# PEER layer on one core: the experts of the first 128 tokens gathered row by row, the dense products run for the other 384

## Chip, cores, metric

One core of one Trainium2 chip. The time is the device time of one execution in microseconds. The kernel before took a median of 5038.12 us over three runs (5035.39 to 5038.38).

## What is computed

Two macaron transformer layers, a mixer of gated delta rule and mLSTM, and then a PEER layer, on 512 tokens of width 1024. The change touches only the PEER layer, which scores product keys, picks 16 experts for each of 8 heads and each token (128 of 16384 experts for a token), and sums their outputs:

```python
def _peer(h, w_q, sub_keys, u_tab, v_tab):          # h: [1, 512, 1024]; u_tab, v_tab: [16384, 1024]
    qry = (t @ w_q).reshape(n_tok, 8, 2, 128)
    scores = jnp.einsum("thpd,hpkd->thpk", qry, sub_keys)              # 128 keys in each half
    s_top, i_top = lax.top_k(scores, 16)
    cand = (s_top[:, :, 0, :, None] + s_top[:, :, 1, None, :]).reshape(n_tok, 8, -1)
    cand_idx = (i_top[:, :, 0, :, None] * 128 + i_top[:, :, 1, None, :]).reshape(n_tok, 8, -1)
    best, pos = lax.top_k(cand, 16)
    idx, gate = jnp.take_along_axis(cand_idx, pos, axis=-1), jax.nn.softmax(best, axis=-1)
    # per block of 128 tokens (tb, ib, gb):
    act = jax.nn.gelu(jnp.einsum("td,thkd->thk", tb, u_tab[ib]), approximate=False)
    out = jnp.einsum("thk,thkd->td", gb * act, v_tab[ib])
```

## The kernel before

Activations lie transposed: eight tiles `x[m]` of 128 features by 512 tokens. Every product with weights goes through `lin` (line 93): one 512 KB load of weights on SyncE's queue (`raw`, 3 buffers), a split into a high and a low float32r part (`wh` by ScalarE at line 82, `wl` by VectorE at line 83, 3 buffers each), and 24 matmuls of 128x128 weights against 512 columns (8 slices of the depth, and for each high by high, high by low, low by high), collected in one PSUM bank. Below, a **lin** is one such set of 24 matmuls.

The PEER layer runs in three stretches.

- **Keys** (`topk`, lines 1481 to 1493): 16 lins for the queries, the key scores, and VectorE's search for the top 16.
- **Pairs** (lines 1497 to 1553): for each of four tiles of 128 tokens, the top 16 of 256 sums for each head, the two key numbers and the gate of each pair (`res`), and then the gate matrix: for each token a 128x128 product of two one-hot tiles (`lt` by VectorE, `rt` by ScalarE and GpSimd), copied by ScalarE into `stage` and stored to DRAM as `gate_d`, so that a token's 16384 gates are zero except at its experts. While this goes on, the first 32 of the 128 blocks of 128 experts have their activations computed ahead (`ahead`, one lin each) and left in DRAM.
- **Dense** (lines 1442 to 1469): 16 groups of 8 expert blocks, 4 to 15 first and then 0 to 3. For each block one lin against `pu`, then VectorE multiplies by 1/rms (`t`, line 1428), ScalarE applies gelu (line 1430), GpSimd multiplies by the gates (`act`, line 1456), ScalarE and VectorE split the product (`eh`, `el`, 11 buffers). For each of 8 output tiles one lin against `pv` with these as moving operand, and VectorE adds the result to `x` (line 1464). The last four groups load their activations and need only the 8 `pv` lins.

In all 128 `pu` and 128 `pv` lins. Each engine runs its instructions in the order of one list; a scheduler draws up that list from program order, so the lists, not the source, tell what stands behind what.

## Time and profile before

| | us |
|---|---|
| median of 3 runs | 5038.12 |
| span of the profiled execution, first to last instruction | 5030.3 |
| around the span (the median less the span; the profiled execution has no time of its own beside the span) | 7.8 |
| TensorE busy in the span | 4827.2 |
| PEER, keys (3300 to 3415) | 115 |
| PEER, pairs (3415 to 3800) | 385 |
| PEER, dense (3800 to 5014) | 1214 |
| final norm and store (5014 to 5030) | 16 |

The stages are cut by hand where the lines of the chain that ended last change from one part of the code to the next. Busy time of TensorE counts matmuls that overlap, each with a modelled end, so a high share says that it is never without work, and the distance between starts says how fast it goes.

### The profile page before, as it was taken

To read this page: it belongs to the slowest core of one execution; us is meant where nothing else is said; L and a number is where in the kernel's file an instruction comes from. 1 tells how busy PE (TensorE), PEld (TensorE's weight loads), DVE (VectorE), ACT (ScalarE), POOL (GpSimd) and SP (SyncE) were. 2 spreads that over 40 slices of the span, in tenths; PEclk is the share of its full clock that TensorE was granted. 3 is DMA by queue.
4 is the path that set the end of the run, shared out by engine and by line. 5 is a ranking of instruction groups with operands and counts; after the bars stand their busy time and mean duration, and the time that the engine had idled before them with its cause. 6 is when DMAs were issued, how large, how long until landed. Compare 5 with 4: busy or idle time off the path is not lost. (4 is left out here: it accounts for less than half of the span.)

```text
span 5030.3 us, 63501 instructions
## 1 busy us (share of the span) xinstructions
PE 4827.2 (96%) x23313; PEld 3957.2 (79%) x23313; DVE 3015.1 (60%) x5922; ACT 2024.4 (40%) x3525; POOL 917.8 (18%) x868
## 2 busy tenths in 40 slices
PE   9999989999999999899999989888899999999998
PEld 7888777788888887777887878767677888888887
DVE  4457877644544587876444678679884444344454
ACT  3235556522322365564223323226784323232332
POOL 0001022200000010223001012234662112121132
PEclk9999999999999999999999999999999999999999
DMA  3334233533323342325233331333445433334353
GB/s 126 96 112 132 78 96 85 174 93 95 100 93 96 113 128 75 106 86 168 94 96 114 115 120 35 99 98 132 149 169 164 130 113 117 126 113 130 113 194 99
DMA packets 256981, 575.05 MB, mean 114 GB/s; under 512 B 28224, under 2 KB 96480, under 8 KB 252576
## 3 DMA queue, kind: packets, MB, share of 16 engines
q1 hardware_dynamic: 256672, 570.99, 35.9%
q8 instruction: 186, 3.05, 0.2%
q14 instruction: 123, 1.01, 0.1%
HBM read 469.31 MB, written 78.53 MB: 109 GB/s over the span
## 5 line engine op out<-in xcount | busy, mean ns | idle before, releaser
L82 ACT CAST wh<-raw 128x1024 fp32r<-128x1024 f32 (+3 forms) x773 | 766.9, 993 | 1964.9 <-PE bk L101 1450.8
L101 PE MATMUL bk<-hh,wh 128*128 128x512 f32 x3016 | 1191.6, 395 | 12.8 <-ACT hh L225 9.2
L101 PE MATMUL bk<-hh,wl 128*128 128x512 f32 x3016 | 1189.6, 394 | 1.7 <-POOL wl L83 1.5
L101 PE MATMUL bk<-hl,wh 128*128 128x512 f32 x3016 | 1188.4, 394 | 0.3 <-DVE hl L226 0.3
L83 DVE TENSOR_TENSOR wl<-raw,wh 128x1024 fp32r<-128x1024 f32 (+3 forms) x693 | 822.3, 1188 | 140.1 <-ACT wh L82 133.2
L101 PEld LDWEIGHTS bk<-hh,wh 128*128 128x128 f32 x3016 | 571.5, 189 | 130.4 <-ACT hh L225 9.6
L101 PEld LDWEIGHTS bk<-hh,wl 128*128 128x128 f32 x3016 | 570.5, 189 | 118.1 <-POOL wl L83 1.9
L101 PEld LDWEIGHTS bk<-hl,wh 128*128 128x128 f32 x3016 | 571.1, 189 | 116.4 <-issue 2.4
L101 PE MATMUL bk<-eh,wh 128*128 128x512 f32 x1024 | 403.0, 394 | 2.8 <-ACT eh L90 2.8
L101 PE MATMUL bk<-el,wh 128*128 128x512 f32 x1024 | 403.5, 394 | 0.8 <-DVE el L91 0.5
L101 PE MATMUL bk<-eh,wl 128*128 128x512 f32 x1024 | 400.1, 391 | 0.0
L1456 POOL TENSOR_TENSOR act<-act,gt 128x512 f32<-128x512 f32 x128 | 224.2, 1759 | 955.1 <-ACT act L1430 813.6
L191 POOL TENSOR_TENSOR sq<-sq,sqt 128x512 f32<-128x512 f32 x62 | 103.7, 1673 | 1212.2 <-ACT sqt L187 1192.0
L1464 DVE TENSOR_TENSOR x<-bk,x 128x512 f32<-128x512 f32 x128 | 88.4, 691 | 371.1 <-PE bk L101 371.1
L83 POOL TENSOR_TENSOR wl<-raw,wh 128x1024 fp32r<-128x1024 f32 (+2 forms) x80 | 185.7, 2322 | 575.4 <-ACT wh L82 455.8
L101 PE MATMUL bk<-gh,wh 128*128 128x512 f32 x704 | 274.4, 390 | 0.0
L101 PE MATMUL bk<-gl,wh 128*128 128x512 f32 x704 | 274.3, 390 | 0.0
L101 PE MATMUL bk<-gh,wl 128*128 128x512 f32 x704 | 274.3, 390 | 0.0
L101 PEld LDWEIGHTS bk<-eh,wh 128*128 128x128 f32 x1024 | 193.0, 188 | 46.3 <-ACT eh L90 3.6
L101 PEld LDWEIGHTS bk<-el,wh 128*128 128x128 f32 x1024 | 193.2, 189 | 43.4 <-DVE el L91 3.2
L101 PEld LDWEIGHTS bk<-eh,wl 128*128 128x128 f32 x1024 | 192.8, 188 | 42.4
L250 DVE TENSOR_TENSOR t<-bk,rr 128x512 f32<-128x512 f32 x88 | 60.8, 691 | 269.1 <-PE bk L101 269.1
(681 smaller groups left out, 8339.5 us busy)
## 6 DMA issues: line engine op xcount, KB each, us to landing
raw<-in_wi SPq DMA_DIRECT2D x176, 512.0 KB, 3.7
raw<-in_pu SPq DMA_DIRECT2D x128, 512.0 KB, 3.5
raw<-in_pv SPq DMA_DIRECT2D x128, 512.0 KB, 3.6
gate_d<-stage SPq DMA_DIRECT2D x32, 1024.0 KB, 3.9
gt<-gate_d SPq DMA_DIRECT2D x16, 2048.0 KB, 9.7
raw<-in_wo SPq DMA_DIRECT2D x64, 448.0 KB, 3.3
raw<-in_mg SPq DMA_DIRECT2D x48, 512.0 KB, 3.7
raw<-in_wo SPq DMA_DIRECT2D x32, 512.0 KB, 3.5
```

The source lines that it names most:

```text
L82: self.nc.scalar.copy(wh[:, :n], raw[:, :n])
L83: (eng or self.nc.vector).tensor_sub(wl[:, :n], raw[:, :n], wh[:, :n].bitcast(F))
L101: self.nc.tensor.matmul(ps, x[:, c], y[k], start=(n == 0), stop=(n == 3 * kk - 1))
L191: nc.gpsimd.tensor_add(self.sq, self.sq, t)
L250: nc.vector.tensor_mul(t2, pb, rr)
L1456: nc.gpsimd.tensor_mul(av, av, gt[:, :, e, :])
L1464: nc.vector.tensor_add(self.x[m], ps, self.x[m])
```

## The change

The first tile of 128 tokens leaves the dense path. `SPT` is 128 and `DW` is 384, the columns that stay.

- Every `pu` and `pv` lin has 384 moving columns in place of 512, and so have `t`, `act`, `eh`, `el`, the gate tile `gt`, the stored activations and the addition to `x`. The weights, their loads and their splits stay as they are: 256 lins, 512 KB each.
- No gate matrix is built for the first tile: its 32 steps of `rt`, `lt`, four matmuls and a copy to `stage`, and its stores, are gone. In their place its expert numbers are written as integers (`eidx`) beside the gates (`egate`). The `ahead` calls that hung on that tile's blocks go with them, so that 26 lins are asked for during the pairs and 6 after them, where it was 30 and 2.
- `by_token` writes the normed activations of those tokens with a token on each partition (`ht`, 128x1024): ScalarE copies, eight transposes.
- `gathered` runs through the 128 experts of each token in steps of four: four indirect DMAs on GpSimd's queue fetch for each token its row of `pur` (128 rows of 4 KB, 512 KB in all), VectorE multiplies each with `ht` and sums (`dot`), ScalarE applies gelu to the four, VectorE multiplies by the gates, then four more indirect DMAs fetch the rows of `pvr` and VectorE adds each, scaled, to `acc`. All 256 fetched tiles `er` share 4 buffers. The tables `pur` and `pvr` are new inputs in the reference's own layout.
- In the last group `acc` is transposed and added to the first 128 columns of `x`.

```diff
-                ps = self.lin(a["pu"][j], 8, hh, hl, eng)
-                t1 = mp.tile([128, 512], F, name="t1", bufs=2)
-                nc.vector.tensor_mul(t1, ps, rr)
-                act = mp.tile([128, 512], F, name="act", bufs=4)
+                ps = self.lin(a["pu"][j], 8, hh, hl, eng, cols=dn)
+                t1 = mp.tile([128, DW], F, name="t1", bufs=2)
+                nc.vector.tensor_mul(t1, ps, rr[:, dn])
+                act = mp.tile([128, DW], F, name="act", bufs=4)
...
+    def gathered(self, ht):
+        nc, mp, a = self.nc, self.mp, self.a
+        NB = 4
+        acc = mp.tile([128, D], F, name="acc")
...
+        def fetch(table, s):
+            r = mp.tile([128, D], F, name="er", tag="er", bufs=4)
+            nc.gpsimd.indirect_dma_start(r, None, a[table], bass.IndirectOffsetOnAxis(ap=self.eidx[:, s:s + 1], axis=0))
+            return r
+        for b in range(0, 128, NB):
+            dot = mp.tile([128, NB], F, name="dot", bufs=2)
+            for i in range(NB):
+                r = fetch("pur", b + i)
+                nc.vector.tensor_tensor_reduce(out=r, in0=r, in1=ht, scale=1.0, scalar=0.0, op0=OP.mult, op1=OP.add,
+                                               accum_out=dot[:, i:i + 1])
+                if i == NB - 1:
+                    w = mp.tile([128, NB], F, name="ew", bufs=2)
+                    nc.scalar.activation(w, dot, AF.Gelu)
+                    nc.vector.tensor_mul(w, w, self.egate[:, b:b + NB])
+                yield
+            for i in range(NB):
+                r = fetch("pvr", b + i)
+                nc.vector.scalar_tensor_tensor(acc, r, w[:, i:i + 1], acc, op0=OP.mult, op1=OP.add)
+                yield
...
                         wh.append(h)
                         wl.append(q)
+                        more(0 if last else 2 if e % 4 == 0 else 1)
+                    if g == groups[-2]:
+                        more(256)
                     for m in range(8):
...
-                        ps = self.lin(a["pv"][g, m], 8, wh, wl)
-                        nc.vector.tensor_add(self.x[m], ps, self.x[m])
-                        if g == groups[-1]:
+                        ps = self.lin(a["pv"][g, m], 8, wh, wl, cols=slice(0, DW))
+                        x = self.x[m][:, dn]
+                        nc.vector.tensor_add(x, ps[:, 0:DW], x)
+                        more(0 if g >= groups[-2] else 1)
...
+            if s0 < 0:
+                nc.vector.scalar_tensor_tensor(res[0], res[0], 128.0, res[1], op0=OP.mult, op1=OP.add)
+                nc.vector.tensor_copy(self.eidx, res[0].rearrange("p h k -> p (h k)"))
+                nc.vector.tensor_copy(self.egate, g.rearrange("p h k -> p (h k)"))
+                continue
```

`more(n)` takes n steps of `gathered`. In program order that is 18 fetches for each group of 8 blocks. The engines' lists are denser: by VectorE's list 12 of the 256 fetched tiles are used before the last `lt` of the pairs, and then 30 for each group of 8 `pu` and 8 `pv` lins, so that all are used up a little past the eighth group and the rest of the dense stretch has none.

VectorE's list in the pairs of the first tile, from the gates of its pairs on, before (line 1525 writes the normed gates, line 1530 copies the transposed lists, line 1549 makes `lt`):

```order
L1525 TENSOR_TENSOR res_30291<-res_30291,gz 128x128 [waits DVE_49]
L83 TENSOR_TENSOR wl<-raw,wh 128x1024 [waits DMAHW5_49]
L1530 COPY sel_28978<-pt 128x128 [waits PE_49]
L1530 COPY sel_28979<-pt 128x128
L1530 COPY sel_28980<-pt 128x128
L1532 TENSOR_SCALAR sel_28981<-pt 128x128
L1549 TENSOR_SCALAR lt<-io,sel_28978,sel_28980 128x128 [waits DVE_49]
L1549 TENSOR_SCALAR lt<-io,sel_28978,sel_28980 128x128 x3
L1428 TENSOR_TENSOR t_30433<-bk,rr 128x512 [waits Activation_49]
L83 TENSOR_TENSOR wl<-raw,wh 128x1024 [waits DMAHW7_49,Activation_49]
```

The same place in the changed kernel (lines 1606 to 1608 write the expert numbers and the gates; line 1486 is `t` of a lin ahead, line 1414 the search of the next tile):

```order
L1608 COPY egate<-res_30329 128x128 [waits DVE_49]
L1607 CAST eidx<-res_30327 128x128 [waits DVE_49]
L1486 TENSOR_TENSOR t_30384<-bk,rr 128x384 [waits PE_49]
L1486 TENSOR_TENSOR t_30420<-bk,rr 128x384 [waits PE_49]
L85 TENSOR_TENSOR wl<-raw,wh 128x1024 [waits DMAHW3_49,Activation_49]
L1414 MAX best<-cand 128x8 [waits Pool_49]
L1414 MAX best<-cand 128x8
```

The copies and the 128 `lt` of the first tile are gone, and the search for the next tile follows at once.

VectorE's list in the middle of the dense stretch, before, at a run of `pv` lins (line 1464 adds a finished lin to `x`, line 83 splits the weights of a later one; the brackets name the semaphores waited for):

```order
L1464 TENSOR_TENSOR x<-bk,x 128x512 [waits PE_49]
L83 TENSOR_TENSOR wl<-raw,wh 128x1024 [waits DMAHW5_49,DVE_49,Activation_49]
L1464 TENSOR_TENSOR x<-bk,x 128x512 [waits PE_49]
L83 TENSOR_TENSOR wl<-raw,wh 128x1024 [waits DMAHW6_49,DVE_49,Activation_49]
L1464 TENSOR_TENSOR x<-bk,x 128x512 [waits PE_49]
L83 TENSOR_TENSOR wl<-raw,wh 128x1024 [waits DMAHW0_49,Activation_49]
L1464 TENSOR_TENSOR x<-bk,x 128x512 [waits PE_49]
```

The same kind of place in the changed kernel (line 1535 is the addition, line 85 the split, lines 1450 and 1459 use a fetched tile, DMASW is the arrival of a fetch, and the `ISA` of one column hands out the sum):

```order
L1535 TENSOR_TENSOR x<-bk,x 128x384 [waits PE_49]
L85 TENSOR_TENSOR wl<-raw,wh 128x1024 [waits DMAHW6_49,Activation_49]
L1455 TENSOR_TENSOR ew<-ew,egate 128x4 [waits Activation_49]
L1459 SCALAR_TENSOR_TENSOR acc<-er,ew,acc 128x1024 [waits DMASW4_49,DVE_49]
L1459 SCALAR_TENSOR_TENSOR acc<-er,ew,acc 128x1024 [waits DMASW5_49,DVE_49]
L1535 TENSOR_TENSOR x<-bk,x 128x384 [waits PE_49]
L85 TENSOR_TENSOR wl<-raw,wh 128x1024 [waits DMAHW7_49,Activation_49]
L1459 SCALAR_TENSOR_TENSOR acc<-er,ew,acc 128x1024 [waits DMASW6_49,DVE_49]
L1450 ISA er,dot<-er,ht 128x1024 [waits DMASW0_49]
L1450 ISA dot 128x1
L1535 TENSOR_TENSOR x<-bk,x 128x384 [waits PE_49]
```

Between the splits of two lins there stand now two operations on fetched tiles, each waiting for its own fetch.

GpSimd's list in the dense stretch, before:

```order
L1456 TENSOR_TENSOR act<-act,gt 128x512 [waits DMAHW4_49,DMAHW3_49,DMAHW5_49,DMAHW2_49,DMAHW6_49,DMAHW1_49,DMAHW7_49,DMAHW0_49,Activation_49]
L1456 TENSOR_TENSOR act<-act,gt 128x512 [waits DMAHW4_49]
L1456 TENSOR_TENSOR act<-act,gt 128x512 [waits Activation_49] x6
L1456 TENSOR_TENSOR act<-act,gt 128x512 [waits DMAHW7_49,Activation_49]
L1456 TENSOR_TENSOR act<-act,gt 128x512 [waits Activation_49] x7
L1456 TENSOR_TENSOR act<-act,gt 128x512 [waits DMAHW3_49,Activation_49]
L1456 TENSOR_TENSOR act<-act,gt 128x512 [waits Activation_49] x7
```

And in the changed kernel (line 1515 multiplies by the gates; line 1444 issues a fetch, which waits until VectorE has done with the tile four fetches earlier):

```order
L1515 TENSOR_TENSOR act<-act,gt 128x384 [waits DMAHW5_49,Activation_49,Pool_49]
L1444 DMA er<-in_pvr,eidx 128x1024 [waits DVE_49] x2
L1515 TENSOR_TENSOR act<-act,gt 128x384 [waits Activation_49,Pool_49]
L1444 DMA er<-in_pur,eidx 128x1024 [waits DMASW4_49,DMASW0_49,DVE_49]
L1444 DMA er<-in_pur,eidx 128x1024 [waits DMASW5_49,DMASW1_49,DVE_49]
L1515 TENSOR_TENSOR act<-act,gt 128x384 [waits Activation_49,Pool_49]
L1444 DMA er<-in_pur,eidx 128x1024 [waits DMASW6_49,DMASW2_49,DVE_49]
L1515 TENSOR_TENSOR act<-act,gt 128x384 [waits Activation_49,Pool_49]
L1444 DMA er<-in_pur,eidx 128x1024 [waits DMASW7_49,DMASW3_49,DVE_49]
L1444 DMA er<-in_pvr,eidx 128x1024 [waits DVE_49]
L1515 TENSOR_TENSOR act<-act,gt 128x384 [waits Activation_49,Pool_49]
```

Fetches stand now ahead of nearly every multiplication by the gates, and a fetch that waits holds up the multiplication behind it.

## Rows read from the trace of the kernel before

**Rows 1.** The page: span, and busy time of each engine.

```profile
span 5030.3 us, 63501 instructions
PE 4827.2 (96%) x23313; PEld 3957.2 (79%) x23313; DVE 3015.1 (60%) x5922; ACT 2024.4 (40%) x3525; POOL 917.8 (18%) x868
```

**Rows 2.** Busy time by stretch: first tile's pairs, all pairs, dense, one late group.

```profile
core 0: us, PE busy (x) PEld busy (x) DVE busy (x) ACT busy (x) POOL busy (x), PEclk, DMA share, GB/s
3415.00:3534.00 119.00, 106.22 (x559) 84.86 (x558) 109.81 (x322) 83.06 (x159) 61.66 (x69) 0.96 0.42 150
3415.00:3800.00 385.00, 345.51 (x1880) 273.97 (x1879) 331.81 (x923) 297.81 (x595) 233.86 (x268) 0.96 0.43 157
3800.00:5014.00 1214.00, 1209.39 (x5289) 994.64 (x5287) 521.76 (x567) 365.96 (x454) 233.85 (x134) 1.00 0.41 128
4786.00:4830.00 44.00, 43.93 (x192) 35.84 (x191) 23.44 (x21) 12.47 (x15) 14.48 (x9) 1.00 0.58 186
```

**Rows 3.** Waits, dense stretch (3834 to 4784): total us, times, longest.

```profile
ACT wh L82 <- PE bk L101: 506.8, 174, 5.7
DVE x L1464 <- PE bk L101: 274.4, 88, 4.7
```

**Rows 4.** TensorE's timeline, dense: first and last of 37 matmuls in a row.

```profile
3899.65 0.39 PE L101 MATMUL bk<-hl,wh 128*128 128x512 f32 x1
...
3907.81 0.39 PE L101 MATMUL bk<-hl,wh 128*128 128x512 f32 x1
```

**Rows 5.** TensorE's timeline, MLA: first and last of 29 matmuls in a row.

```profile
1934.75 0.34 PE L117 MATMUL pt<-wh,latl 128*128 128x384 f32 x1
...
1939.70 0.33 PE L117 MATMUL pt<-wl,lath 128*128 128x384 f32 x1
```

**Rows 6.** Groups by form, dense (3834 to 4784): busy us, mean ns of one.

```profile
L83 DVE TENSOR_TENSOR wl<-raw,wh 128x1024 fp32r<-128x1024 f32 x174 | 213.2, 1225 | 28.4 <-ACT wh L82 28.4
L82 ACT CAST wh<-raw 128x1024 fp32r<-128x1024 f32 x174 | 182.8, 1051 | 506.8 <-PE bk L101 506.8
L1456 POOL TENSOR_TENSOR act<-act,gt 128x512 f32<-128x512 f32 x86 | 154.8, 1800 | 798.3 <-ACT act L1430 798.3
L91 DVE TENSOR_TENSOR el<-act,eh 128x512 fp32r<-128x512 f32 x85 | 58.9, 692 | 156.2 <-ACT eh L90 156.2
```

**Rows 7.** Groups by form, pairs (3415 to 3800).

```profile
L1549 DVE TENSOR_SCALAR lt<-io,sel,sel 128x128 f32<-128x128 f32 x512 | 144.0, 347 | 37.4 <-PE g L1550 36.5
L1551 ACT COPY stage<-g 128x512 f32<-128x512 f32 x128 | 134.0, 1047 | 10.8 <-PE g L1550 10.6
L1541 ACT ACTIVATE rt<-io,sel 128x128 f32<-128x128 f32 x256 | 87.7, 396 | 3.0 <-DVE sel L1532 3.0
L1545 ACT ACTIVATE rt<-rt 128x256 f32<-128x256 f32 x128 | 53.8, 420 | 1.6
L83 DVE TENSOR_TENSOR wl<-raw,wh 128x1024 fp32r<-128x1024 f32 x35 | 42.5, 1215 | 0.9 <-ACT wh L82 0.9
L1517 POOL TENSOR_TENSOR eq<-eq,sif 128x2048 f32<-128x2048 f32 x8 | 36.6, 4580 | 57.2 <-DVE eq L1516 57.2
L1412 DVE MATCH_VALUE_LOAD pos<-best,scr 128x8 f32 x32 | 2.6, 80 | 0.1
```

**Rows 8.** Timelines of VectorE and GpSimd just ahead of PEER: start us, us.

```profile
3282.58 0.74 DVE L226 SCALAR_TENSOR_TENSOR hl<-x,vec,hh 128x512 fp32r<-128x512 f32 x1
...
3286.88 3.51 DVE L226 SCALAR_TENSOR_TENSOR hl<-x,vec,hh 128x512 fp32r<-128x512 f32 x2 [0.97 <-ACT hh L225]
...
3285.78 2.36 POOL L83 TENSOR_TENSOR wl<-raw,wh 128x1024 fp32r<-128x1024 f32 x1 [1.02 <-ACT wh L82]
3288.11 1.74 POOL L191 TENSOR_TENSOR sq<-sq,sqt 128x512 f32<-128x512 f32 x1
```

**Rows 9.** DMA: issues (KB, us to landing), one issue on SyncE, the fullest 8 us.

```profile
raw<-in_pu SPq DMA_DIRECT2D x88, 512.0 KB, 3.5
gt<-gate_d SPq DMA_DIRECT2D x10, 2048.0 KB, 9.7
3919.89 0.53 SPq L1449 DMA_DIRECT2D gt<-gate_d  x1
3924.00:3932.00 8.00, 8.00 (x36) 6.58 (x35) 2.13 (x3) 1.05 (x1) 0.00 (x0) 1.00 1.08 355
```

More of the change, by code (lines that the diff above doesn't have):

```diff
@@ L30 @@
 TB = 16
+SPT = 128
+DW = 512 - SPT
 EARLY = 4
@@ L91, in hilo, with lin @@
         self.nc.vector.tensor_sub(lo, src, hi.bitcast(F))
-    def lin(self, ap, kk, hh, hl, eng=None, bank="bk"):
+    def lin(self, ap, kk, hh, hl, eng=None, bank="bk", cols=None):
         wh, wl = self.weights(ap, kk * 128, eng)
         ps = self.bank(bank)
+        if cols is not None:
+            hh, hl = ([x[:, cols] for x in y] for y in (hh, hl))
+            ps = ps[:, 0:cols.stop - cols.start]
         n = 0
@@ L1412, in top16, with by_token @@
         nc.vector.max_index(idx[:, 8:16], vals[:, 8:16], scratch)
+    def by_token(self, rc):
+        nc, mp = self.nc, self.mp
+        ht = mp.tile([128, D], F, name="ht")
+        for q in range(2):
+            pt = self.bank("pt")
+            for k in range(4):
+                m = 4 * q + k
+                xg = mp.tile([128, 128], F, name="xg", bufs=2)
+                nc.scalar.activation(xg, self.x[m][:, 0:SPT], AF.Copy, scale=self.vec[:, 56 + m:57 + m])
+                nc.tensor.transpose(pt[:, k * 128:k * 128 + 128], xg, self.idn)
+            nc.scalar.activation(ht[:, q * 512:q * 512 + 512], pt, AF.Copy, scale=rc[:, 0:1])
+        return ht
+    def gathered(self, ht):
+        nc, mp, a = self.nc, self.mp, self.a
+        NB = 4
+        acc = mp.tile([128, D], F, name="acc")
+        nc.gpsimd.memset(acc, 0.0)
+        self.acc = acc
+        def fetch(table, s):
[17 more added lines that the diff above has]
+                yield
     def peer(self):
@@ L1444, in peer @@
                     wh, wl = [], []
+                    last = g == groups[-1]
                     for e in range(8):
@@ L1469, in peer @@
                             self.x[m] = t
-    def topk(self, mp, hh, hl, rr, io, sel, gd, ahead):
-        nc, a = self.nc, self.a
-        keys = []
-        for q in range(4):
-            k = mp.tile([128, 4, 128], F, name="keys", bufs=4)
-            nc.sync.dma_start(k, a["pk"][q])
-            keys.append(k)
-        sv = mp.tile([128, 4, 8, 2, 16], F, name="sv")
-        si = mp.tile([128, 4, 8, 2, 16], U32, name="si")
-        for j in range(16):
-            ps = self.lin(a["pwq"][j], 8, hh, hl, nc.gpsimd)
-            x = mp.tile([128, 512], F, name="qt", bufs=2)
-            nc.vector.tensor_mul(x, ps, rr)
-            ps = self.bank("sc")
-            for t in range(4):
-                c = slice(t * 128, t * 128 + 128)
-                nc.tensor.matmul(ps[:, c], x[:, c], keys[j // 4][:, j % 4], start=True, stop=True)
-            s = mp.tile([128, 512], F, name="sc", bufs=2)
-            nc.scalar.copy(s, ps)
-            for t in range(4):
-                w = mp.tile([128, 128], F, name="scr", bufs=2)
-                self.top16(sv[:, t, j // 2, j % 2], si[:, t, j // 2, j % 2], s[:, t * 128:t * 128 + 128], w)
-        sif = mp.tile([128, 4, 8, 2, 16], F, name="sif")
-        nc.vector.tensor_copy(sif, si)
@@ new lines, in topk @@
+    def topk(self, sp, hh, hl, rr, io, sel, gd, ahead):
+        nc, tc, a = self.nc, self.tc, self.a
+        sv = sp.tile([128, 4, 8, 2, 16], F, name="sv")
+        sif = sp.tile([128, 4, 8, 2, 16], F, name="sif")
+        with tc.tile_pool(name="topk1", bufs=1) as mp:
+            si = mp.tile([128, 4, 8, 2, 16], U32, name="si")
+            keys = []
+            for q in range(4):
+                k = mp.tile([128, 4, 128], F, name="keys", bufs=4)
+                nc.sync.dma_start(k, a["pk"][q])
+                keys.append(k)
+            for j in range(16):
+                ps = self.lin(a["pwq"][j], 8, hh, hl, nc.gpsimd)
+                x = mp.tile([128, 512], F, name="qt", bufs=2)
+                nc.vector.tensor_mul(x, ps, rr)
+                ps = self.bank("sc")
+                for t in range(4):
+                    c = slice(t * 128, t * 128 + 128)
+                    nc.tensor.matmul(ps[:, c], x[:, c], keys[j // 4][:, j % 4], start=True, stop=True)
+                s = mp.tile([128, 512], F, name="sc", bufs=2)
+                nc.scalar.copy(s, ps)
+                for t in range(4):
+                    w = mp.tile([128, 128], F, name="scr", bufs=2)
+                    self.top16(sv[:, t, j // 2, j % 2], si[:, t, j // 2, j % 2], s[:, t * 128:t * 128 + 128], w)
+            nc.vector.tensor_copy(sif, si)
+        with tc.tile_pool(name="topk2", bufs=1) as mp:
+            self.pairs(mp, sv, sif, io, sel, gd, ahead)
@@ L1496, in topk, with pairs @@
+    def pairs(self, mp, sv, sif, io, sel, gd, ahead):
+        nc = self.nc
         b3, b4 = [128, 8, 16], [128, 8, 16, 16]
@@ L1498, in topk @@
             ahead((6, 4, 4, 4)[t])
+            s0 = t * 128 - SPT
             cand = mp.tile(b4, F, name="cand", tag="big", bufs=2)
```

40 lines of the change are left out of this document (30 added, 10 removed).

## The prediction

> **What bounds the kernel now.** The page comes first: TensorE is busy 96% of the span, VectorE 60% [rows 1]. Where the time goes in PEER is read from the busy time by stretch [rows 2]. In the dense stretch TensorE is busy 1209 of 1214 us, and in a late group, which has only 8 lins, 43.9 of 44 us. In the pairs nothing is full: TensorE's 346, VectorE's 332 and ScalarE's 298 us out of 385 overlap and wait for each other in turn. The waits confirm the dense reading [rows 3]: ScalarE's split waits 507 us for a lin to give a buffer back, VectorE's addition 274 us for a lin to end. Everybody waits for TensorE. So in the dense stretch a shorter lin is worth its whole length, until something else becomes the slowest; in the pairs a saving is worth what it takes off several engines at once.
>
> **A lin of 384 columns.** Matmuls of 512 columns start every (3907.81 - 3899.65) / 36 = 226.7 ns [rows 4]. The kernel already runs float32r matmuls of 384 columns with a new weight load each, in MLA, and these start every (1939.70 - 1934.75) / 28 = 176.8 ns [rows 5]. The weight load that stays 128 wide does not eat the saving. A lin takes 950 us / 174 = 5.46 us [rows 6], 0.02 over 24 spacings; with 384 columns 24 x 0.1768 + 0.02 = 4.27. Saved: 1.19 us each.
>
> **Pairs, 385 us.** The first tile's 32 steps go. On ScalarE a step is 1.047 + 2 x 0.396 + 0.420 = 2.26 us [rows 7], 72 us in all. On VectorE it is four `lt`, 128 x 0.281 = 36 us (144.0 / 512), with some 12 us for six lins that leave the stretch (a split of 1.2 and a `t` of 0.7 each); 12 fetched tiles at about 1.3 us come, 16 us. So VectorE loses about 32 of its 332 us, a tenth, or 37 us if the stretch shrinks in proportion. The first tile's own 119 us had VectorE busy for 110 [rows 2], so it can't give up ScalarE's whole 72. Ends 37 and 72; I take 55, between them, since neither engine bounds the stretch alone.
>
> **By-token copy and the last addition.** Eight small and two 512-wide copies on ScalarE, idle for most of the keys, and eight transposes on TensorE at both ends: 2 us.
>
> **Dense, if the fetches cost nothing.** Of 256 lins the pairs held 35 [rows 7], so 221 fill the 1214 us. After, six more come late: 227 x 4.27 = 969 us, a gain of 245. Span 5030.3 + 2 - 55 - 245 = 4732, and 7.8 around it: 4740 us. A group of 16 lins would take 68.3 us.
>
> **What the fetches cost.** By the lists 244 of the 256 fetched tiles are used in the dense stretch at 30 a group, for 244 / 30 = 8.13 groups. What fills such a group, engine by engine:
> - VectorE: 16 splits at 1.225 = 19.6 [rows 6]. 24 operations on 384 columns (`t`, `el`, `x`): from 692 ns at 512 and 1225 at 1024, 559 ns each, 13.4 us. 15 scaled additions: 0.74 at 512 columns alone [rows 8], so 1.27 at 1024, 19.1 us. 15 multiply-and-sums, an operation that the trace does not have: the same operands as the split, 1.225, and a second small instruction, 0.08 like the small one in [rows 7]; 19.6 us. At half that rate it would be 2.3, which adds 16 us. I take the first, as its form is nearest. Sum 71.7 us, already over 68.3.
> - VectorE and GpSimd together: one `hl` takes 0.74 us alone, two take 3.51 us while GpSimd runs 2.36 and 1.74 us of its own two-operand work [rows 8]. They wait for each other. GpSimd's 8 gate products, 1.80 x 384/512 = 1.35 us each, 10.8 us, meet a VectorE whose time is 87% two-operand work on SBUF: up to 9.4 us. Sum 81. The Trainium skill (SBUF — State Buffer, Who interferes with whom) says that a VectorE instruction with two SBUF inputs contends with a GpSimd instruction that reads SBUF, and not with one that only writes. The trace agrees as far as [rows 8] go; no run here shows whether issuing fetches counts.
> - DMA: 46 tiles of 0.524 MB and a gate tile of 1.57 MB, 25.7 MB. The fullest 8 us moved 355 GB/s [rows 9], so 72 us.
> - GpSimd: 10.8 us and 30 fetch issues of unknown price. The lower end is an issue on SyncE, 0.53 us [rows 9]; the upper the longest GpSimd operation of this layer, 4.58 [rows 7]. I take 1.3, that of a small tile's work, between a gate product and the lower end: 50 us, hidden. The Trainium skill (DMA: Bandwidth & Descriptors, SWDGE vs HWDGE vs iDMA) has GpSimd's cores write the descriptors in software, and under Latency gives about 1 us to the first byte; no run here shows it. By that, as an estimate, 41 us, hidden too.
> - The ring of four: a tile is busy from issue to the end of its use, 3.5 to 9.7 us to land [rows 9], 1.3 to be used, and about 3 of waiting in the two lists (an estimate, most of a lin). A quarter of it is 2.0 to 3.5 us a fetch, 59 to 105 us a group.
>
> Four of these lie near 70 and share in-order lists: VectorE's splits stand behind uses that wait for fetches, and gate products behind fetches that wait for VectorE. I take VectorE's 81 and 3 us for such waits: **84 us a group**, 8.13 x (84 - 68.3) = 128 us. Span 4860, time **4868 us**. Against the profiled span and the same 7.8 around it, this is the median of before less 170. What is late next in those groups is TensorE, which waits for `wl`; after them and in the last four groups it is the bound again, at 34 us a late group for 44.
>
> **The rivals.**
> - *The fetches hide entirely.* GpSimd issues far enough ahead, the gate products don't collide, VectorE keeps up at 72 or less: 4740 to 4770. For it: before, VectorE's splits lose almost nothing to GpSimd (1225 ns beside it, [rows 6]). Against it: the sum of 71.7 is above 68.3 without any wait, and DMA needs the same. 0.14.
> - *Slower than before: the fetch is paced by GpSimd's list or the ring.* The gain without fetches is 298 us, and 298 / 8.13 = 36.7, so at 105 us a group, 3.5 us a fetch, the change is worth nothing. On GpSimd that is an issue of (105 - 10.8) / 30 = 3.1 us; at 4.58 a group takes 148 us and the time would be 4740 + 8.13 x 80 = 5390. On the ring it is landing at 9.7, which a 2 MB load takes [rows 9]; a fetch is a quarter of it, and rows of 4 KB like a load of weights, which speaks against it. What speaks for it: nothing in the trace tells the price of 128 addresses taken from a tile. 0.16.
> - *VectorE's new operations run at half rate.* Group of about 100 us, 4998; it is within the first forecast's upper part.
> - *The matmuls don't get shorter.* Excluded by [rows 5], which is the same type and weight load.
>
> **Chances and range.** Between 72 and 98 us a group, 4770 to 4980: 0.62, the forecast's own range. Hidden: 0.14. Between 98 and 105, still faster: 0.05. No change: 0.03. Slower: 0.16. What this kernel's runs can tell from no change is about 0.2%, 10 us. Faster is then 0.62 + 0.14 + 0.05 = 0.81. The range 4720 to 5020 reaches down to the hidden case with more than 55 us won in the pairs, and up to a paced fetch just short of no gain; outside it stay the slower case and a few in a hundred below.
>
> **What would show it.** In the changed profile matmuls of line 101's successor start every 177 ns while TensorE is fed; the late groups take about 34 us; the pairs end about 55 us earlier. In the first eight groups TensorE's waits are for `wl`, VectorE is busy over 85%, DMA moves about 300 GB/s. If TensorE is busy throughout there, the fetches hide. If VectorE waits for DMA of `er` most of the time and GpSimd is busy or its queue waits, the pace of the fetch decides, and I am wrong by the distance of that pace from 2.8 us. If the multiply-and-sum lasts 2.3 us, that term is mis-sized.

## The result: 4869.8 us against 5037.3, and the profile after

The changed kernel takes 4869.8 us (median of 4 runs, 4865.1 to 4870.8), the kernel before 5037.3 (median of 4, 5035.4 to 5038.4). The ratio is 0.9668, 95% interval 0.9654 to 0.9681: 167.5 us less. The prediction was 4868.

The page of the profile after, its span and the busy time of each engine, stands against [rows 1]:

```profile
span 4867.3 us, 63592 instructions
PE 4532.7 (93%) x23070; PEld 3875.8 (80%) x23070; DVE 3264.9 (67%) x6217; ACT 1948.5 (40%) x3439; POOL 1127.8 (23%) x1061
```

The span is 163 us shorter, but TensorE's busy time fell by 295: it is idle for 335 us now, where it was for 203. VectorE gained 250 us of work. The busy time by stretch shows where; it answers to [rows 2]. The stretches are the pairs, seven whole groups of experts with fetched tiles, and one late group:

```profile
core 0: us, PE busy (x) PEld busy (x) DVE busy (x) ACT busy (x) POOL busy (x), PEclk, DMA share, GB/s
3415.00:3762.00 347.00, 272.48 (x1615) 244.94 (x1614) 313.69 (x824) 237.01 (x468) 213.55 (x220) 0.90 0.48 164
3842.51:4434.49 591.98, 509.69 (x2692) 479.06 (x2691) 500.45 (x624) 174.31 (x251) 321.38 (x267) 0.95 0.88 304
4716.00:4750.00 34.00, 33.92 (x192) 33.41 (x192) 20.52 (x24) 11.52 (x15) 9.25 (x9) 1.00 0.66 211
```

The pairs take about 347 us, a late group 34. In the seven groups, 591.98 / 7 = 84.6 us each, TensorE is busy 86%, VectorE 500.45 / 591.98 = 85%, and the DMA engines 88% at 304 GB/s. TensorE's timeline has this pace where it is fed, the first and the last of 53 matmuls in a row, for [rows 4] and [rows 5]:

```profile
4499.68 0.34 PE L106 MATMUL bk<-el,wh 128*128 128x384 f32 x1
...
4508.86 0.34 PE L106 MATMUL bk<-eh,wl 128*128 128x384 f32 x1
```

(4508.86 - 4499.68) / 52 = 176.5 ns. The groups by form in the same seven groups, for [rows 6]: the two operations on fetched tiles, the weights' split, the fetches' issues and the gate product:

```profile
L1459 DVE SCALAR_TENSOR_TENSOR acc<-er,ew,acc 128x1024 f32<-128x1024 f32 x106 | 148.5, 1401 | 24.4 <-DMA er<-in_pvr,eidx 23.3
...
L85 DVE TENSOR_TENSOR wl<-raw,wh 128x1024 fp32r<-128x1024 f32 x112 | 147.3, 1315 | 16.4 <-ACT wh L84 16.1 <-issue 0.4
...
L1450 DVE CUSTOM_DVE_ANT_0 er<-er,ht 128x1024 f32<-128x1024 f32 x105 | 139.2, 1332 | 36.9 <-DMA er<-in_pur,eidx 36.8
...
L1444 POOL DMA_INDIRECT er<-in_pvr,eidx x106 | 137.2, 1295 | 92.0 <-DVE dot L1450 57.2 <-DVE acc L1459 23.2 <-issue 8.4
...
L1444 POOL DMA_INDIRECT er<-in_pur,eidx x105 | 115.5, 1100 | 173.0 <-DVE acc L1459 119.4 <-DVE dot L1450 35.8 <-DMA er<-in_pvr,eidx 9.1
...
L1515 POOL TENSOR_TENSOR act<-act,gt 128x384 f32<-128x384 f32 x56 | 70.6, 1261 | 5.9 <-ACT act L1488 2.9 <-issue 2.2
```

And the waits there, for [rows 3] (total us, times, longest):

```profile
POOL er L1444 <- DVE acc L1459: 142.5, 83, 10.2
...
ACT eh L92 <- POOL act L1515: 92.6, 56, 2.9
...
PE bk L106 <- ACT eh L92: 41.5, 14, 3.8
...
DVE er L1450 <- DMA er<-in_pur,eidx: 36.8, 18, 6.5
...
PE bk L106 <- DVE wl L85: 27.9, 39, 1.8
...
DVE acc L1459 <- DMA er<-in_pvr,eidx: 23.3, 15, 2.6
```

Before, everybody waited for TensorE. Now GpSimd waits for VectorE to free a fetched tile (143 us for the sums alone); TensorE waits for ScalarE's split of the activations (42 us; I had named only the weights' `wl`, 28 us); and VectorE waits for rows that have not landed, 36.8 + 23.3 = 60 us or 8.6 a group. The split follows the gate product, which stands in GpSimd's list among the fetches. The 93 us that ScalarE waits for that product are no sign of the fetches by themselves: 13.2 us a group, and the kernel without fetches below has 14.0.

TensorE also ran slower where it had been starved. In the changed kernel it was busy for 5.8 of the 12 us from 4216 to 4228, and its granted clock fell to 0.50, the lower of its two levels (1.2 and 2.4 GHz). Two stretches of 4 us in which it was busy throughout, just after that and a little later:

```profile
4228.00:4232.00 4.00, 4.00 (x15) 4.00 (x14) 3.75 (x4) 0.25 (x2) 1.61 (x2) 0.55 1.01 308
...
4236.00:4240.00 4.00, 4.00 (x25) 4.00 (x24) 1.29 (x1) 1.05 (x1) 0.29 (x1) 1.00 1.03 403
```

It did 15 matmuls in the first and 25 in the second. Counted over the timeline of the seven groups, 140 of its 2690 matmuls start 0.25 to 0.36 us after the one before, in place of 0.177. That is 2.5 us a group, and 0.3 in the kernel without fetches, whose groups are 17.3 us shorter; the rest of the difference is TensorE's waiting.

The chain that ended last shows how long a fetch takes from issue to landing when it is waited for (two of its 25 rows of fetches, start and us):

```profile
4139.86 10.96 DMA er<-in_pur,eidx
...
4183.50 7.31 DMA er<-in_pur,eidx
```

### The profile page after: what moved, and what is told of

Same layout as the page of the kernel before. It is cut to its first block, busy times and chain, and to the rows that moved or that the text cites. A ratio compares the mean times of both kernels' runs of the same rounds, so it can differ in the third digit from the quotient of the medians.

```text
span 4867.3 us, 63592 instructions
## 1 busy us (share of the span) xinstructions
PE 4532.7 (93%) x23070; PEld 3875.8 (80%) x23070; DVE 3264.9 (67%) x6217; ACT 1948.5 (40%) x3439; POOL 1127.8 (23%) x1061
## 5 line engine op out<-in xcount | busy, mean ns | idle before, releaser
L106 PE MATMUL bk<-hh,wh 128*128 128x512 f32 (+1 forms) x3016 | 1138.6, 378 | 47.7 <-DVE t L1486 19.0
L106 PE MATMUL bk<-hh,wl 128*128 128x512 f32 (+1 forms) x3016 | 1136.3, 377 | 37.0 <-DVE wl L85 36.0
L106 PE MATMUL bk<-hl,wh 128*128 128x512 f32 (+1 forms) x3016 | 1135.0, 376 | 0.3 <-DVE hl L231 0.3
L85 DVE TENSOR_TENSOR wl<-raw,wh 128x1024 fp32r<-128x1024 f32 (+3 forms) x693 | 842.0, 1216 | 155.5 <-ACT wh L84 148.5
L106 PE MATMUL bk<-eh,wh 128*128 128x384 f32 x1024 | 355.5, 349 | 55.6 <-ACT eh L92 53.1
L106 PE MATMUL bk<-el,wh 128*128 128x384 f32 x1024 | 356.0, 348 | 9.5 <-DVE el L93 9.2
L106 PE MATMUL bk<-eh,wl 128*128 128x384 f32 x1024 | 353.0, 345 | 2.2 <-DVE wl L85 2.0
L1515 POOL TENSOR_TENSOR act<-act,gt 128x384 f32<-128x384 f32 x128 | 168.2, 1320 | 291.1 <-ACT act L1488 174.8
L264 DVE SCALAR_TENSOR_TENSOR x<-bk,x 128x512 f32<-128x512 f32 x96 | 66.4, 692 | 231.6 <-PE bk L106 231.6
```

Source lines behind the costliest of these rows:

```text
L85: (eng or self.nc.vector).tensor_sub(wl[:, :n], raw[:, :n], wh[:, :n].bitcast(F))
L106: self.nc.tensor.matmul(ps, x[:, c], y[k], start=(n == 0), stop=(n == 3 * kk - 1))
L264: nc.vector.scalar_tensor_tensor(self.x[m], ps, 0.5, self.x[m], op0=OP.mult, op1=OP.add)
L1515: nc.gpsimd.tensor_mul(av, av, gt[:, :, e, :])
```

## Experiments

The theory from the trace was that VectorE's own work decides a group with fetched tiles. Its rival was the fetch: transfers, the ring of four tiles, landing, GpSimd's issues. All times of a group below are from the start of one addition to `x` to the start of the same addition some whole groups later. `keep_in_program_order` keeps an instruction, in its engine's list, where the program has it; without it the scheduler moves it. The changed kernel's code asks for 10 uses a group, all beside the activations, and the scheduler listed 30, 16 of them beside the activations and 14 beside the sums. (The description of the change has 18 in program order. That is wrong: `groups[-2]` is 2, so `g >= groups[-2]` holds in all twelve whole groups, and nothing is asked for beside their sums.)

| kernel | uses a group | us a group | VectorE busy, us | median us |
|---|---|---|---|---|
| changed | 30 | 84.6 | 71.5 | 4870 |
| no_fetch | 0 | 67.3 | 33.5 | 4725 |
| half_fetch | 30, 15 fetches | 77.8 | 72.0 | 4825 |
| pin30 | 30 | 105.4 | 71.3 | 5057 |
| half_dve_pin30 | 30, half as wide | 95.6 | 57.5 | 4970 |
| spread21 | 21 | 75.1 | 57.6 | 4840 |
| spread30 | 30 | 86.3 | 72.3 | 4884 |
| half_dve_spread30 | 30, half as wide | 77.4 | 53.6 | 4831 |
| ring6ep | 30 | 84.7 | 71.4 | 4889 |
| gate_dve | 27 | 76.5 | 66.1 | 4803 |
| gate_dve_spread21 | 21 | 68.0 | 59.0 | 4761 |
| gate_dve_spread19 | 19 | 67.8 | 56.7 | 4773 |

### no_fetch

```diff
-            rows = self.gathered(ht)
+            self.acc = mp.tile([128, D], F, name="acc")
+            nc.gpsimd.memset(self.acc, 0.0)
+            rows = iter(())
```

> The 256 fetches and the 256 VectorE operations on fetched tiles are left out (the sum over the first 128 tokens' experts is a tile of zeros, so their expert output is missing). Both theories: the matmuls of 384 columns and the shorter pairs are left, and TensorE bounds the dense stretch at 68.3 us a group of 16 lins. By the prediction's terms 4740 us; with the 33 us that the pairs gave in place of the 55 that I took, 4762. What is above this in the changed kernel, 4870 less this time, is what the fetches cost; I expect 105 to 130 us of it. If it is below 4740 or above 4780, one of the terms without fetches is mis-sized.

Measured: 4725.5 us, ratio to before 0.938 (0.9363 to 0.9396). Eleven groups, busy time by stretch:

```profile
3821.99:4562.35 740.36, 738.36 (x4226) 732.05 (x4225) 368.86 (x448) 271.03 (x360) 152.92 (x95) 1.00 0.49 151
```

TensorE is busy 738 of 740 us, 67.3 a group. So the fetches and what VectorE does with them cost 4870 - 4725 = 144 us, and everything else in the prediction was 15 us too dear. TensorE's matmuls do not wait for ScalarE's split of the activations here, though ScalarE waits for the gate product as long as ever, 14.0 us a group:

```profile
ACT eh L92 <- POOL act L1517: 153.9, 90, 1.8
```

### half_fetch

```diff
-            r = mp.tile([128, D], F, name="er", tag="er", bufs=4)
+            r = self.ep.tile([128, D], F, name="er", tag="er", bufs=3)
...
-                r = fetch("pur", b + i)
-                nc.vector.tensor_tensor_reduce(out=r, in0=r, in1=ht, scale=1.0, scalar=0.0, op0=OP.mult, op1=OP.add,
+                if i % 2 == 0:
+                    r = fetch("pur", b + i)
+                junk = self.ep.tile([128, D], F, name="junk", bufs=1)
+                nc.vector.tensor_tensor_reduce(out=junk, in0=r, in1=ht, scale=1.0, scalar=0.0, op0=OP.mult, op1=OP.add,
...
-                r = fetch("pvr", b + i)
+                if i % 2 == 0:
+                    r = fetch("pvr", b + i)
```

> Every fetched tile is used twice, so 128 fetches are issued and moved in place of 256; VectorE's 256 operations stay (the multiply-and-sum writes to a tile of its own, and the ring has three tiles in place of four, each used twice; the output is that of wrong experts for every other one). Theory 1, VectorE's time and its collisions with GpSimd set the 85 us of a group with 30 uses: the operations are the same, so 80 to 85 us a group and 4830 to 4870 us. Theory 2, the fetch side sets it (landing time over the ring, transfers, GpSimd's issues): half as many fetches, the group falls to TensorE's 68 to 72 us, 4760 to 4790.

Measured: 4825.4 us (0.9581, 0.9563 to 0.9598), just under the range of theory 1 and far above that of theory 2. Seven groups:

```profile
3839.14:4383.92 544.78, 497.34 (x2712) 486.04 (x2711) 504.01 (x623) 175.56 (x251) 192.72 (x160) 0.95 0.70 229
```

VectorE is busy 504 of 545 us, 93%. With half the fetches its work is nearly the whole group, 72.0 of 77.8 us; the fetches that were left out, their transfers, landing and issues together, are worth 84.6 - 77.8 = 6.8 us a group.

### pin30 and half_dve_pin30

```diff
-            nc.gpsimd.indirect_dma_start(r, None, a[table], bass.IndirectOffsetOnAxis(ap=self.eidx[:, s:s + 1], axis=0))
+            self.tc.keep_in_program_order(nc.gpsimd.indirect_dma_start(r, None, a[table], bass.IndirectOffsetOnAxis(ap=self.eidx[:, s:s + 1], axis=0)))
...
-                        more(0 if last else 2 if e % 4 == 0 else 1)
+                        more(0 if last else (4, 4, 4, 3, 4, 4, 4, 3)[e])
...
-                        more(0 if g >= groups[-2] else 1)
+                        more(0 if last else 0)
```

The second kernel also has `[:, 0:512]` on the operands of VectorE's two operations on fetched tiles.

> The same work as the changed kernel, with each fetch's issue kept behind the instructions that stand ahead of it in GpSimd's list, and all 30 uses of a group asked for beside its eight activations; the lists still hold 30 uses a group. It is the control of the next kernel. Both theories: 4860 to 4880, as the changed kernel; a difference is what the order alone makes.

> As the kernel before it, but VectorE's operations on fetched tiles take 512 of the 1024 columns (half of each dot product and half of each sum are left out); all 256 fetches are issued and moved whole. Theory 1, VectorE's time: a use falls from 1.3 to about 0.75 us, a group's VectorE work from 75 to 56 us, under TensorE's 68.3: 4760 to 4790. Theory 2, the fetch side: the fetches are the same, 80 to 85 us a group, 4840 to 4870.

Measured: 5056.9 us (1.0038, 1.0026 to 1.0051) and 4969.5 (0.9863, 0.9841 to 0.9885). Both miss. The same 256 fetches, asked for and kept in other places, give back the whole gain of the change. In pin30's list 23 to 28 of a group's 30 uses now stand beside the activations and 2 to 7 among the sums. Seven groups of pin30 by stretch:

```profile
3874.15:4611.61 737.46, 541.16 (x2690) 514.63 (x2689) 498.82 (x621) 175.47 (x251) 338.82 (x266) 0.83 0.73 245
```

A wait of pin30 (total us, times, longest) says why that is dear, in six groups:

```profile
POOL act L1515 <- issue: 200.5, 6, 36.6
```

Once a group GpSimd stands still for some 33 us: its next instruction is a gate product of the next group, and every fetch is kept behind it, so none is issued while TensorE does the sums. If a half group of sums takes 34 us as in the late groups, the half with the activations is left with 105.4 - 34 = 71 us. TensorE is starved often enough there for a granted clock of 0.83 in the mean; counted as above, slow spacings make 5.7 us a group. The half-width kernel has the same hole, so it can't tell the theories apart. The next kernels spread the uses.

### spread21, spread30 and half_dve_spread30

```diff
-                nc.vector.tensor_tensor_reduce(out=r, in0=r, in1=ht, scale=1.0, scalar=0.0, op0=OP.mult, op1=OP.add,
-                                               accum_out=dot[:, i:i + 1])
+                self.tc.keep_in_program_order(nc.vector.tensor_tensor_reduce(
+                    out=r, in0=r, in1=ht, scale=1.0, scalar=0.0, op0=OP.mult, op1=OP.add, accum_out=dot[:, i:i + 1]))
...
-                nc.vector.scalar_tensor_tensor(acc, r, w[:, i:i + 1], acc, op0=OP.mult, op1=OP.add)
+                self.tc.keep_in_program_order(nc.vector.scalar_tensor_tensor(acc, r, w[:, i:i + 1], acc, op0=OP.mult, op1=OP.add))
...
-                        more(0 if last else 2 if e % 4 == 0 else 1)
+                        more(0 if last else (2, 1, 1, 2, 1, 1, 2, 1)[e])
...
-                        more(0 if g >= groups[-2] else 1)
+                        more(0 if last else (1, 1, 2, 1, 1, 1, 2, 1)[m])
```

This is spread21; in the other two the tuples are eight twos and `(1, 2, 2, 2, 1, 2, 2, 2)`, and the half-width one has `[:, 0:512]` on the operands of VectorE's two operations. The fetches are free to be listed ahead of their uses.

> The changed kernel's work, with VectorE's uses of fetched tiles kept in the order in which they are asked for: 21 a group over twelve groups, 12 beside the activations and 9 beside the sums, in place of 30 a group over eight. Theory 1, VectorE's time per group decides: nine uses less at about 1.25 us take its 72 busy us to 61, below the 67.3 that TensorE needs in the kernel without fetches; 68 to 72 us a group, 4740 to 4790 us. Theory 2, each fetch costs the group a fixed wait whatever the density (a late fetch stops VectorE's list): 256 fetches times the 0.57 us that one costs now (145 us over 256), so 4850 to 4880.

> The control of spread21: uses kept in order too, but 30 a group, 16 beside the activations and 14 beside the sums, as many as the changed kernel lists. Both theories: 80 to 88 us a group, 4840 to 4890 us. If it is as fast as spread21, the keeping in order and not the density is what helps; if it is as slow as the kernel with all thirty beside the activations, 5057, the keeping in order is what hurts.

> As spread30, with VectorE's operations on fetched tiles on 512 of the 1024 columns (half of each dot product and of each sum is left out); all fetches issued and moved whole. Theory 1, VectorE's time: 15 us less or more a group, to about 56 busy, so TensorE's pace of 67 to 71 us a group and 4740 to 4780. Theory 2, the fetch: 30 fetches at the 2.1 us that they took in the activation halves of the half-width kernel before ((97 - 34) / 30) are 62 us, hidden only if they are spread as well as that; waits for landing in VectorE's list stay, so 75 to 82 us a group and 4790 to 4850.

Measured: spread21 4839.8 us (0.9606, 0.959 to 0.9622), spread30 4884.0 (0.9696, 0.9679 to 0.9712), half_dve_spread30 4831.1 (0.9595, 0.9577 to 0.9611). Nine groups of spread21, six of spread30, six of the half-width one, by stretch:

```profile
3928.16:4604.01 675.85, 630.51 (x3464) 618.86 (x3463) 518.07 (x669) 223.94 (x313) 338.29 (x261) 0.96 0.81 280
```

```profile
3851.60:4369.12 517.52, 440.04 (x2314) 425.95 (x2313) 433.71 (x531) 150.67 (x215) 303.62 (x228) 0.91 0.86 299
```

```profile
3902.10:4366.21 464.11, 422.23 (x2291) 410.85 (x2292) 321.62 (x536) 149.73 (x215) 282.47 (x228) 0.95 0.93 331
```

The control, spread30, is near the changed kernel, 86.3 us a group for 84.6, so keeping the uses in order is not what helps. Two things follow. From 30 to 21 uses a group loses 86.3 - 75.1 = 11.2 us, less than the 72.3 - 57.6 = 14.7 that VectorE's work falls by: its idle time grows from 14.0 to 17.5. And the half-width kernel, with VectorE at 53.6 us a group, still needs 77.4, as theory 2 has it: its DMA engines are busy 93%, at 331 GB/s, VectorE waits for rows, and TensorE for the split:

```profile
DVE er L1450 <- DMA er<-in_pur,eidx: 53.9, 37, 3.8
...
PE bk L106 <- ACT eh L92: 31.8, 12, 5.5
...
DVE acc L1459 <- DMA er<-in_pvr,eidx: 27.2, 21, 3.6
```

VectorE's waits for rows are 81 us over six groups, 13.5 each. So at 30 a group the group stays near 77 us both when half of the fetches go and when VectorE's work shrinks, and neither side alone makes the 84.6. That the transfers alone would hold it at 77 is not shown: this kernel still has the gate product among the fetches, and TensorE waits 5.3 us a group for the split behind it. And spread21 missed: VectorE has 57.6 us of work, under TensorE's 67.3, the transfers are at 81%, and the group takes 75.1. Its waits name a third thing:

```profile
ACT eh L92 <- POOL act L1515: 120.7, 72, 3.7
...
DVE el L93 <- ACT eh L92: 80.0, 47, 2.5
...
PE bk L106 <- ACT eh L92: 33.7, 14, 3.8
```

TensorE waits 34 us for ScalarE's split, for which its matmuls never wait without fetches. The other two rows only show the way that the wait takes, from GpSimd's gate product to ScalarE and VectorE; per group they are no longer than in no_fetch (13.4 for 14.0 us, and 8.9 for 11.6), where nobody is late by them.

### ring6ep

```diff
-            r = mp.tile([128, D], F, name="er", tag="er", bufs=4)
+            r = self.ep.tile([128, D], F, name="er", tag="er", bufs=6)
...
-                        h = ep.tile([128, DW], FR, name="eh", bufs=11)
-                        q = ep.tile([128, DW], FR, name="el", bufs=11)
+                        h = ep.tile([128, DW], FR, name="eh", bufs=9)
+                        q = ep.tile([128, DW], FR, name="el", bufs=9)
```

> Six tiles for fetched rows in place of four (in the pool of the expert stage; to make room the ring of split activations has 9 tiles in place of 11). Theory 1a, VectorE's list is full: its 72 busy us and the waits beside them stay, 82 to 86 us a group, 4850 to 4880. Theory 2a, the ring of four makes fetches late, since a fetch is only issued when a use four before it has ended and takes 7 to 11 us to land: the 8.6 us a group in which VectorE waits for a fetched tile fall to 0 to 3, 76 to 79 us a group, 4800 to 4830.

Measured: 4888.5 us (0.9695, 0.9675 to 0.9716), 84.7 us a group. Two more tiles for rows (with two fewer for each part of the split activations) buy nothing: VectorE waits for rows 6.9 us a group for 8.6, and the group is as long. So at this density a longer ring does not help; what the two tiles fewer cost is not separated from it, and the late groups take 36 to 37 us here for 34 to 35.

### gate_dve, gate_dve_spread21 and gate_dve_spread19

```diff
-                        nc.gpsimd.tensor_mul(av, av, gt[:, :, e, :])
+                        nc.vector.tensor_mul(av, av, gt[:, :, e, :])
```

The second and the third keep uses in order as spread21 does. The last one asks for 19 uses a group, and for eight in each of three late groups.

> One line of the changed kernel: the gate product (activation times gate, 8 a group) goes from GpSimd to VectorE; GpSimd then only issues fetches. The list gives 27 uses a group, over some nine groups. Theory A, the coupling costs the group its 13 us above VectorE's 72 busy: a gate product stands in GpSimd's list behind a fetch that waits for VectorE to free a tile, the split of the activations waits for it, and TensorE for that; besides, the products collide with VectorE's work. Without both a group is VectorE's own work: 72 less 3 uses (4), less about 5 of collisions, plus 8 products of 0.55 (4.4), so 67 to 74 us a group and 4740 to 4800. Theory B, VectorE waits for its own work and for landing rows, and 4.4 us more on the fullest engine cost as much: 82 to 88 us a group, 4850 to 4900.

> spread21 with the gate product on VectorE. VectorE then has about 55 + 4.4 = 59 to 60 us of work a group, and TensorE 67.3. Theory A (the coupling makes the 75 us of spread21): 68 to 71 us a group, 4735 to 4780. Theory B (late rows in VectorE's list make them): 74 to 78, 4830 to 4870.

> As the kernel before it, with 19 uses a group and the last 28 or so in three of the four late groups, where VectorE has some 20 of 34 us of work. Theory A: within 15 us of the kernel before it, 4730 to 4780; the late groups stay at 34 to 38 us. Theory B: 4810 to 4860.

Measured: gate_dve 4802.7 us (0.9527, 0.9511 to 0.9543), gate_dve_spread21 4761.1 (0.9452, 0.9436 to 0.9468), gate_dve_spread19 4773.3 (0.947, 0.9454 to 0.9486). Theory A holds in gate_dve_spread21, and in gate_dve_spread19 except that its late groups got longer. gate_dve lies between the theories: 76.5 us a group, where A had 74 at the most and B 82 at the least, and 3 us above A's range. There VectorE is still idle for 76.5 - 66.1 = 10.4 us, 6.2 of them for rows. One line, which gives the fullest engine more instructions, is worth 67 us, but the list also has 27 uses a group for 30; with 21 uses before and after, the line is worth 4840 - 4761 = 79. Eight groups of gate_dve by stretch:

```profile
3835.30:4447.12 611.82, 568.88 (x3091) 548.10 (x3091) 528.83 (x736) 200.09 (x284) 263.59 (x217) 0.97 0.91 316
```

Its groups by form there:

```profile
L85 DVE TENSOR_TENSOR wl<-raw,wh 128x1024 fp32r<-128x1024 f32 x128 | 155.7, 1216 | 22.0 <-ACT wh L84 22.0
...
L1459 DVE SCALAR_TENSOR_TENSOR acc<-er,ew,acc 128x1024 f32<-128x1024 f32 x108 | 138.2, 1280 | 17.6 <-DMA er<-in_pvr,eidx 16.5
...
L1450 DVE CUSTOM_DVE_ANT_0 er<-er,ht 128x1024 f32<-128x1024 f32 x109 | 132.2, 1219 | 35.0 <-DMA er<-in_pur,eidx 33.4 <-issue 1.5
...
L1444 POOL DMA_INDIRECT er<-in_pur,eidx x109 | 137.7, 1264 | 195.6 <-DVE acc L1459 168.6 <-DVE dot L1450 13.6 <-DVE wl L85 6.9
...
L1515 DVE TENSOR_TENSOR act<-act,gt 128x384 f32<-128x384 f32 x64 | 35.2, 550 | 0.0
```

The three large VectorE operations take 1216, 1280 and 1219 ns, where they took 1315, 1401 and 1332, though GpSimd issues 109 and 108 fetches among them; in half_fetch, with half the issues and the gate product on GpSimd, they take 1324, 1403 and 1365. The gate products were what they collided with, not the issues. Nine groups of gate_dve_spread21, by stretch:

```profile
3906.53:4518.94 612.41, 605.88 (x3458) 599.81 (x3457) 530.66 (x742) 223.93 (x313) 244.46 (x189) 1.00 0.89 309
```

TensorE is busy 606 of 612 us: it is the bound again, at 68.0 us a group, and 36 us above the kernel without fetches are left in all. Its longest wait in all nine groups is no longer for the split:

```profile
PE bk L106 <- DVE wl L85: 6.4, 6, 1.5
```

Against spread21, which differs in this line alone, a group is 7.1 us shorter though VectorE has 1.4 us more to do: by the starts of its matmuls TensorE waits 5.1 us less and loses 1.9 less to its lower clock (25 slow spacings for 146). VectorE waits no less for rows, 25 us over the nine groups for 18, so rows that land in time more often are not what helps; fewer collisions take 2.1 us a group off VectorE's work. This is the fastest version, 109 us under the changed kernel. Moving uses to the late groups costs more there (39 to 43 us in three of them, for 34 to 38 expected) than it saves.

### pairs0

```diff
-            ahead((6, 4, 4, 4)[t])
+            ahead((0, 4, 4, 4)[t])
```

> The six lins listed ahead of the first token tile's pairs go to the end of the pairs (ahead of the dense groups); nothing else is moved by hand. It is for one reading: the first copy of a gate step, at 3514.5 us in the changed kernel and 49 us later than before. Theory V, VectorE is what the first two tiles' key selections fill (20 of 20 us in three of the five slices): the first step starts earlier by six splits and six scaled copies, 6 x 1.75 = 10 us. Theory T, TensorE at a granted clock of 0.66 to 0.83 and its lins hold the stretch: earlier by 6 lins of 4.2 us or more, 25 to 40 us. The time of the kernel rises by 5 to 20 us either way, since TensorE has no hole for the lins later.

Measured: 4869.3 us in one run; the first copy of a gate step is at

```profile
3508.52 1.03 ACT L1635 COPY stage<-g 128x512 f32<-128x512 f32 x1 [1.91 <-PE g L1634]
```

6 us earlier than in the changed kernel, and the last one is 9 us earlier (3752.3 for 3761.2). The pairs themselves begin 3 us later in this run (GpSimd's first sums of scores, `cand`, at 3424.9 for 3421.6), so counted from there the first step comes 9 us earlier. Theory T's 25 to 40 is out; theory V's 10 is near. For 20 us between the two selections TensorE now does nothing at all:

```profile
3455.00:3475.00 20.00, 0.00 (x0) 0.00 (x0) 17.51 (x50) 0.00 (x0) 12.13 (x6) 0.53 0.32 105
```

and its granted clock is 0.53 there, near the lower of its two levels; the next step comes earlier all the same. The kernel's time did not rise as expected, and it did not fall: the 9 us are gone by the last addition of the dense stretch (4850.3 for 4850.5), and the lins that left the pairs are done in between.

## Why the prediction was right, point by point

**A lin of 384 columns: right.** 176.5 ns from start to start for 176.8; 67.28 us over 16 lins is 4.205 us a lin for 4.27. A late group takes 34 us.

**Lins in the dense stretch: 224, not 227.** Twelve groups of 16 and four of 8. I had six lins leave the pairs; none did (35 splits there, before and after). With the shorter lin that is 3 x 4.27 + 224 x 0.065 = 27 us less than predicted.

**Pairs: 34 us, not 55. This step failed:** "I take 55, between them, since neither engine bounds the stretch alone". The first copies of two successive tiles' gate steps, before and after:

```profile
3465.15 1.06 ACT L1551 COPY stage<-g 128x512 f32<-128x512 f32 x1 [0.39 <-PE g L1550]
...
3554.92 1.07 ACT L1551 COPY stage<-g 128x512 f32<-128x512 f32 x1
```

```profile
3514.53 1.06 ACT L1635 COPY stage<-g 128x512 f32<-128x512 f32 x1 [1.91 <-PE g L1634]
...
3606.17 1.05 ACT L1635 COPY stage<-g 128x512 f32<-128x512 f32 x1 [1.91 <-PE g L1634]
```

A tile's steps took 65 us (3465.2 to 3529.8), but 90 passed from that tile's first step to the next one's: the steps hid part of the next tile's key selection, which is VectorE's. Without the first tile's steps the two selections stand in a row, and VectorE all but fills them (93 of the 100 us from 3415), while ScalarE fills the steps (busy time by stretch after, two slices of the selections and one of the steps):

```profile
3435.00:3455.00 20.00, 14.93 (x67) 13.84 (x67) 19.97 (x49) 5.19 (x8) 4.62 (x1) 0.83 0.37 109
...
3475.00:3495.00 20.00, 10.78 (x43) 10.27 (x44) 20.00 (x55) 4.11 (x5) 4.92 (x2) 0.66 0.54 180
...
3625.00:3650.00 25.00, 22.62 (x152) 20.04 (x151) 22.25 (x83) 24.68 (x53) 16.68 (x26) 1.00 0.46 180
```

So the second tile's steps begin at 3514.5 for 3554.9, 40 us earlier, and each later tile takes 1 to 3 us more than before, which gives back 6.5: the last step starts at 3761.2 for 3795.1. The bounds of 37 and 72 treated the engines as if each saved its work through the whole stretch; the row of the first tile, with VectorE at 110 of 119 us, had it.

**Without fetches: 4740 predicted, 4725 measured.** 21 us from the pairs are more than made up by the 27 of the lins; the other 9 or so are not assigned. The fetches were put at 128 us and cost 144. So it is in part luck that 4868 met 4870: one side was 15 us too dear, the other 16 too cheap.

**VectorE's terms: each right, the sum 10 us too high.** Without collisions the scaled addition took 1.280 us for 1.27, the multiply-and-sum 1.219 and 0.08 for 1.225 and 0.08; half rate is out. (Its 4998 us lay above the forecast's own range, which ended at 4980, and not within it.) Collisions are (1315 - 1216) x 16 + (1401 - 1280) x 15 + (1332 - 1219) x 15 = 5.1 us a group, not 9.4. But busy time, collisions included, is 71.5 us, not 81: rows of a timeline overlap by about 0.08 us (4202.91 + 1.21 ends after 4204.05 has begun, in the rows below), some 60 times a group, and I had added durations. One collision, from the timelines of GpSimd and VectorE after:

```profile
4203.69 1.29 POOL L1515 TENSOR_TENSOR act<-act,gt 128x384 f32<-128x384 f32 x1 [0.32 <-issue]
...
4202.91 1.21 DVE L1450 CUSTOM_DVE_ANT_0 er<-er,ht 128x1024 f32<-128x1024 f32 x1
...
4204.05 2.01 DVE L85 TENSOR_TENSOR wl<-raw,wh 128x1024 fp32r<-128x1024 f32 x1
...
4208.31 1.22 DVE L85 TENSOR_TENSOR wl<-raw,wh 128x1024 fp32r<-128x1024 f32 x1
```

The split that begins while the gate product reads takes 2.01 us, one without it 1.22. The Trainium skill (SBUF — State Buffer, Who interferes with whom) calls the ports that the two engines share an exclusive lock and says that the order of issue decides which of them blocks; the trace agrees, as the gate product began first, 4203.69 + 1.29 - 4204.05 is 0.93 and the split lost 0.79. The section exempts GpSimd instructions that only write SBUF; the issues, which cost VectorE nothing in gate_dve, agree with that, unless taking the 128 addresses counts as a read.

**Waits: 13, not 3.** Of 84.6 us VectorE is idle for 13.1, of which 8.6 for rows. This term and the one before it were wrong by about 10 us each in opposite directions, and that 81 + 3 = 84 met 84.6 was luck. The mechanism was told in one sentence ("VectorE's splits stand behind uses that wait for fetches, and gate products behind fetches that wait for VectorE") and priced at 3. Two runs show that this is a term of its own: half_fetch, where VectorE's work stays at 72.0 us and its idle time falls to 5.8, and gate_dve_spread21 against spread21, where its work rises by 1.4 and its idle time falls from 17.5 to 9.0. TensorE's lower clock, 2.5 us a group, is nowhere in the prediction.

**Which limit: partly wrong.** I took VectorE's time to decide. It does so where half of the fetches are gone (72.0 of 77.8 us). In the changed kernel it is 71.5 of 84.6, and the landing of rows and the way that the in-order lists of GpSimd, ScalarE and VectorE pass on each other's waits add the rest; how much of the 13.1 is each one's no run says. DMA's 72 us was not reached (25.7 MB a group; 304 GB/s after, 331 at most over whole groups, which is 78 us). GpSimd's issue, 1.1 to 1.3 us for 1.3, was right; that the ring does not pace it is what ring6ep suggests.

**The rivals.** "Hidden entirely" did not happen, but gate_dve_spread21 comes within 36 us of it. The slower rival was right about its place, not about this kernel: at 105.4 us a group pin30 is slower than before, 0.4%, at the break-even of 105, because of where GpSimd's list lets fetches be issued.

## What to carry to other kernels

Work that is moved to an idle engine joins that engine's list. If the list also holds instructions that wait for a third engine, as GpSimd's fetches do for VectorE's tiles, products behind them can be late, and moving one short instruction to the busier engine can be worth more than its time. Spread added work so that the slowest engine of each half group stays under the bound, and price waits between lists apart from busy time: busy time from sums over a stretch, not from added durations. Where TensorE waits, count also what its lower clock costs after the wait.
